# mLSTM heads of a hybrid decoder layer: column sums of a folded tile by transposes and a free-axis sum, in place of products with a constant

## The chip, the cores and the metric

The kernel runs on one core of one Trainium2 chip, in a single launch. The metric is device time in microseconds (us), from the start to the end of one execution; smaller is better.

## The reference, cut to what matters

One decoder layer on x of shape (1, 1024, 1024), everything in float32. Half of the first mixing stage is an mLSTM with four heads of width 128; the other half is an attention with forget gates (eight heads of width 64). Cross-attention, a squared-ReLU MLP and a last norm follow. The change lies in what each mLSTM head does at its end:

```python
den = scores.sum(-1) + inter * jnp.einsum('bhd,bhtd->bht', n, qc)
h = num / jnp.maximum(jnp.abs(den), jnp.exp(-m_t))[..., None]
...
mh = mh * lax.rsqrt(jnp.mean(mh * mh, axis=-1, keepdims=True) + EPS)
```

For each of the 1024 time steps a head needs two sums: one for the denominator `den`, one of the squares of the 128 numerators `num`. From them comes one factor for each time step, by which the numerators are multiplied.

## The kernel before, in words

The names: PE is the matrix engine (TensorE), DVE the VectorE, ACT the ScalarE, POOL the GpSimd, SP the queue that issues the transfers. Nearly every product is in float32 cut into two parts (`wh`, `wl` for weights, a pair of `act` tiles for data), and takes three matmuls (`mm3`, L221 to L223). PSUM has eight banks, of which three are called `sc`, two `tp`, and one each `mm`, `m2` (shown as `m`) and `ov`.

A head (`ml_head`, L630) works on two halves `hf` of 512 time steps, numerators lying with the channel on the partition and time on the free axis. For each half it goes over four blocks `j` of 128 keys: scores on PE into an `sc` bank (L655), a decay by ACT (`Exp`, L657) from a row `nmb` that was loaded into the tile `r_a` or `r_y`, a mask by POOL (L659), their product by DVE (L660), a cut of it into `r_d` (ACT, L138) and `r_e` (DVE, L139), the product with the values into the bank `ov` (L666), and a running sum of the denominators on POOL into `r_b` (L664). At the end of a half the sums over partitions are prepared by folding (L673 to L681): the tile `sq` (`r_a` for the first half, `r_y` for the second) holds on its partitions 0 to 63 the denominator terms, both halves of the partitions added, and on 64 to 127 the squares, added likewise. So the two sums wanted for each of 512 time steps are the sums over the lower and over the upper 64 partitions of `sq`.

`sums(hf)` (L636) takes them as four matmuls (one for each 128 time steps) with `sq` as the stationary operand and the constant `halves` [128, 2] as the moving one: column 0 of `halves` is one on the lower partitions, column 1 on the upper. The result is [128 time steps, 2] for each block, eight columns in one bank. ACT takes the absolute value of four of them into `dens` (L640), DVE copies the other four to `sqs` (L641). `sums(0)` is called in the loop of the second half, at j = 6, and `sums(1)` at the end. A dozen small instructions on DVE and one on POOL (L685 to L691, and L233 to L243) make the factor `c_fac` of it, 1024 values in 8 columns.

The rest is called the closing of the head. PE transposes `c_fac` (`to_row`, L285), ACT copies it out (L286), SP stores it in DRAM (`facd`) and loads it back, spread over all partitions, into `r_a` and `r_y` (L289, L696). DVE multiplies the numerators (tiles `r_f`) by it (L700) and by a gate (L701), ACT and DVE cut them, and the parts are stored to `mix` (L704, L705). The tiles are few: `r_a` and `r_y` have one buffer each, `r_f` two. So the next head's `nmb` can be loaded into `r_a` (L645) only when the closing before it has stored `mix` from `r_a`, and its numerators have no place until `r_f` is stored.

Between a head's `sums(1)` and its closing, and among the blocks of the next head, PE has the projections for the next head to do (`ml_project`: conv_silu, fx_project, gate; 24 matmuls of 512 columns each), and after the last head's projections the values of the attention (`token_major` on `w_fv`, 24 matmuls of 256 columns for each of eight tiles). The first stage takes from about 60 to 354 us of the span; then the slots of the attention follow.

The order of the instructions on each engine is not written out in this stage. The framework puts them in order while the program is built, by a timeline that it reckons for itself:

```python
with tile.TileContext(nc, schedule_with_timeline_sim=True) as tc:
```

From the attention's slots on (`in_order`) the order is fixed by the code. Each engine runs its list strictly in that order.

Of the kernel before, what the change touches and what calls it, by code (L numbers as in the profile page):

```python
# [11 lines left out]
AF = mybir.ActivationFunctionType  # L12
ALU = mybir.AluOpType
# [4 lines left out]
P = 128  # L18
# [26 lines left out]
def hybrid_layer(ctx: ExitStack, tc: tile.TileContext, a: dict, out: bass.AP):  # L45
    nc = tc.nc
    v, s, g = nc.vector, nc.scalar, nc.gpsimd
# [39 lines left out]
    def ps_tile(tag):  # L87
        return psum.tile([P, 512], F32, tag=tag, name=name(tag), bufs=PBUFS[tag])

    def sc():  # L90
        return ps_tile("sc")
# [4 lines left out]
    def ov_():  # L96
        return ps_tile("ov")
# [10 lines left out]
    def const(n, shape, dt=F32):  # L108
        return pool.tile(shape, dt, tag=n, name=n, bufs=1)
# [4 lines left out]
    ones = const("ones", [P, 1])  # L114
    g.memset(ones, 1.0)
    ident = const("ident", [P, P])
# [5 lines left out]
    g.affine_select(out=causal, in_=causal, pattern=[[-1, TH]], compare_op=ALU.is_ge, fill=-BIG, base=TH - P, channel_multiplier=1)  # L122
    half = const("half", [P, 8])
    g.memset(half, -0.5)
    halves = const("halves", [P, 2])
    g.memset(halves, 0.0)
    for e in range(2):
        g.memset(halves[e * (P // 2) : (e + 1) * (P // 2), e : e + 1], 1.0)
    vec = const("vec", [P, a["vec"].shape[1]])

    busy = ov_()
# [115 lines left out]
        for t in range(n):  # L247
            nc.tensor.matmul(ps[:, t * P : (t + 1) * P], cols[:, t : t + 1].broadcast_to([P, P]), ident, start=True, stop=True)

    def sum_cols(ps, src, n, by=ones):  # L250
        m = by.shape[1]
        for t in range(n):
            nc.tensor.matmul(ps[:, t * m : (t + 1) * m], src[:, t * P : (t + 1) * P], by, start=True, stop=True)

    def square_sum(acc, x, first, by=s, add=v):
        sq = acc if first else w2("c")[:, : x.shape[-1]]
# [88 lines left out]
    h = [(act(), act()), (act(), act())]  # L345
# [20 lines left out]
    for k in range(KT):  # L366
        if k == 1:
            load(wg_raw, a["w_gate"])
        if k % 2 == 0:
            c = slice(k % 4 * 256, k % 4 * 256 + 512)  # L370
# [39 lines left out]
    z, e, q, lf = (small[:, i:j].rearrange("p (t c) -> p t c", c=c) for i, j, c in ((0, 128, GC), (128, 224, GW), (224, 320, GW), (320, 416, GW)))  # L410
# [54 lines left out]
    ps = ov_()  # L465
# [92 lines left out]
    def quarter(e):  # L558
        return slice(e * HQ, e * HQ + HQ)
# [70 lines left out]
    def ml_head(hd, q, k, og, yq, state, late):  # L630
        fac = col("fac", 8)
        nums, folded = [], []
        dens = col("dens", 8)
        sqs = col("sqs", 8)

        def sums(hf):  # L636
            ps = sc()[:, 0:8]
            sum_cols(ps, folded[hf], 4, halves)
            ps = ps.rearrange("p (t e) -> p e t", e=2)
            s.activation(dens[:, 4 * hf : 4 * hf + 4], ps[:, 0], AF.Abs)  # L640
            v.tensor_copy(sqs[:, 4 * hf : 4 * hf + 4], ps[:, 1])  # L641

        for hf in range(2):
            nmb = w2("ay"[hf])
# [4 lines left out]
            for j in range(4 * hf, last + 1):  # L649
                d0 = j - 4 * hf  # L650
                c = quarter(d0 // 2)
# [17 lines left out]
                if j == 0:  # L669
                    e = w2("c", HQ)  # L670
# [6 lines left out]
            c = slice(0 if hf else HQ, TH)  # L677
# [7 lines left out]
        v.tensor_tensor(out=dens, in0=dens, in1=emc[:, :, hd], op=ALU.max)  # L685
        rd = col("rd", 8)
        v.reciprocal(rd, dens)
        v.tensor_tensor(out=sqs, in0=sqs, in1=rd, op=ALU.mult)
        v.tensor_tensor(out=sqs, in0=sqs, in1=rd, op=ALU.mult)
        rsqrt_cols(fac, sqs, 1.0 / P, 8)  # L690
        v.tensor_tensor(out=fac, in0=fac, in1=rd, op=ALU.mult)  # L691
# [82 lines left out]
    for _ in range(2):  # L774
        t = act().rearrange("p a b -> p (a b)").rearrange("p (i c) -> p i c", i=4)
# [272 lines left out]
    raws_, ages, cuts_, halves, last_raw = [], [], {}, [0], []  # L1048
# [139 lines left out]
    n = 0  # L1188
# [39 lines left out]
    for n0 in (0, 4):  # L1228
        ws = [weights(a["w_out_b"][n0 // 2 + i], 6 * P) for i in range(2)]
        for hf in range(2):  # L1230
            for n in range(n0, n0 + 4):
                w = both(ws[n // 2 % 2], lambda t: t.rearrange("p (k c) -> p k c", k=3)[:, :, n % 2 * P : n % 2 * P + P])
                ps = mm()
# [331 lines left out]
    for hd in range(XH):  # L1565
        q = query_blocks(hd)
        if hd == 0:
            t = act()
            for n in range(4):
                oh[n], ol[n] = t[:, n], t[:, 4 + n]  # L1570
        elif hd > 1:
            t = last_room if hd == 2 else right_room("-")
            t = t.rearrange("p q k c -> p (q k c)").rearrange("p (q n c) -> p q n c", q=2, n=2)
# [214 lines left out]
    for at, (b, m) in enumerate(steps):  # L1788
# [33 lines left out]
    for i in range(2):  # L1822
        t = act()
# [123 lines left out]
```

## Time and profile before

| | |
|---|---|
| median of 3 runs | 1497.02 us (1496.89 to 1497.15) |
| profiled execution | 1498.83 us, span of its instructions 1497.1 us |
| mean granted TensorE clock | 0.998 of full speed |
| busy | PE 99%, weight loads 84%, DVE 76%, ACT 52%, POOL 35% |

The profile is of one execution. Its views name groups by line, engine and operation, `out<-in` by the tile's names; times in a timeline are us from the start of the span. A matmul's recorded duration reaches beyond the start of the next one, since matmuls are pipelined; what a matmul costs is the distance between two starts. A matmul of two float32 operands appears as two records, a transposition as one.

### The profile page before, as it was taken

The page shows a single profiled execution, that of the slowest core. Times are in us where ns is not written, and L with a number is a line of the kernel's source. Part 1 is how long each engine was busy: PE and PEld are TensorE (multiplying, and loading weights), DVE is VectorE, ACT ScalarE, POOL GpSimd, SP SyncE. Part 2 cuts the span into 40 slices and gives each one's busy share as a digit, 9 for nine tenths or more (in the row PEclk, how much of TensorE's full clock was granted, in tenths as well). Part 3 has the DMA queues.
Part 4 walks back from the last instruction along what each step waited for, and adds up shares of the span by engine and source line. Part 5 has one row for each costly group of instructions (what it writes and reads, how often), then busy time and mean ns, then how long its engine had stood idle before and what let it go on. Part 6 is the DMA issues. An engine that isn't in the chain of part 4 may idle for free. (4 is left out here: it accounts for less than half of the span.)

```text
span 1497.1 us, 22496 instructions
## 1 busy us (share of the span) xinstructions
PE 1479.4 (99%) x7790; PEld 1253.1 (84%) x7790; DVE 1131.0 (76%) x1867; ACT 773.1 (52%) x1492; POOL 521.2 (35%) x552
## 2 busy tenths in 40 slices
PE   9999999999999999999999999999999999999997
PEld 9988888889999888889988787888888888888887
DVE  7775776776798875677668888999996677787665
ACT  7434353445688664577644557666665521222134
POOL 1002020414456441633200045454544365553312
PEclk9999999999999999999999999999999999999999
DMA  6422333446778867744544447776678767776623
GB/s 231 138 95 69 130 97 134 132 132 191 247 242 284 285 231 247 261 168 128 167 165 155 139 171 268 253 246 238 233 267 304 264 260 281 281 274 253 250 87 113
DMA packets 125878, 303.58 MB, mean 203 GB/s; under 512 B 14898, under 2 KB 30060, under 8 KB 118852
## 3 DMA queue, kind: packets, MB, share of 16 engines
q1 hardware_dynamic: 125764, 302.15, 57.9%
q8 instruction: 61, 1.00, 0.3%
q14 instruction: 53, 0.43, 0.1%
HBM read 203.28 MB, written 98.82 MB: 202 GB/s over the span
## 5 line engine op out<-in xcount | busy, mean ns | idle before, releaser
L221 PE MATMUL tp<-act,wl 128*128 128x512 f32 (+1 forms) x440 | 172.7, 392 | 0.0
L222 PE MATMUL tp<-act,wh 128*128 128x512 f32 (+1 forms) x440 | 172.2, 391 | 0.0
L223 PE MATMUL tp<-act,wh 128*128 128x512 f32 (+1 forms) x440 | 171.7, 391 | 0.0
L139 DVE TENSOR_TENSOR wl<-wr,wh 128x1024 fp32r<-128x1024 f32 (+2 forms) x99 | 131.8, 1331 | 29.0 <-ACT wh L138 28.7
L138 ACT ACTIVATE wh<-wr 128x1024 fp32r<-128x1024 f32 (+2 forms) x99 | 99.9, 1010 | 86.3 <-PE tp L223 28.9
L221 PE MATMUL mm<-act,wl 128*128 128x512 f32 (+1 forms) x332 | 123.7, 373 | 0.0
L223 PE MATMUL mm<-act,wh 128*128 128x512 f32 (+1 forms) x332 | 123.5, 372 | 0.0
L222 PE MATMUL mm<-act,wh 128*128 128x512 f32 (+1 forms) x332 | 123.5, 372 | 0.0
L221 PE MATMUL m<-act,wl 128*128 128x512 f32 (+1 forms) x308 | 113.9, 370 | 1.8 <-DVE wl L139 1.8
L223 PE MATMUL m<-act,wh 128*128 128x512 f32 (+1 forms) x308 | 113.7, 369 | 0.0
L222 PE MATMUL m<-act,wh 128*128 128x512 f32 (+1 forms) x308 | 113.4, 368 | 0.0
L223 PE MATMUL sc<-act,wh 128*128 128x512 f32 (+1 forms) x280 | 105.6, 377 | 0.0
L221 PE MATMUL sc<-act,wl 128*128 128x512 f32 (+1 forms) x280 | 105.5, 377 | 0.0
L222 PE MATMUL sc<-act,wh 128*128 128x512 f32 (+1 forms) x280 | 105.5, 377 | 0.0
L223 PEld LDWEIGHTS tp<-act,wh 128*128 128x128 f32 x440 | 82.7, 188 | 18.6
L221 PEld LDWEIGHTS tp<-act,wl 128*128 128x128 f32 x440 | 82.7, 188 | 18.5 <-DVE r_f L1627 0.2
L222 PEld LDWEIGHTS tp<-act,wh 128*128 128x128 f32 x440 | 82.8, 188 | 18.2
L1711 POOL TENSOR_TENSOR z<-wr 128x256 f32<-128x256 f32 x56 | 50.1, 915 | 135.6 <-DMA wr<-w_ff2q 133.1
L138 ACT ACTIVATE wh<-z 128x1024 fp32r<-128x1024 f32 (+1 forms) x54 | 55.4, 1026 | 79.0 <-POOL z L1711 58.4
L139 DVE TENSOR_TENSOR wl<-z,wh 128x1024 fp32r<-128x1024 f32 (+1 forms) x54 | 79.3, 1468 | 9.3 <-ACT wh L138 9.3
L138 ACT ACTIVATE w<-wr 128x768 fp32r<-128x768 f32 (+3 forms) x35 | 28.1, 802 | 109.5 <-PE tp L221 33.5
L223 PEld LDWEIGHTS mm<-act,wh 128*128 128x128 f32 x332 | 62.4, 188 | 11.7
(793 smaller groups left out, 4398.5 us busy)
## 6 DMA issues: line engine op xcount, KB each, us to landing
act<-right SPq DMA_DIRECT2D x49, 1024.0 KB
right<-w SPq DMA_DIRECT2D x56, 256.0 KB
wr<-w_ff2q SPq DMA_DIRECT2D x28, 512.0 KB
right<-r_d SPq DMA_DIRECT2D x49, 256.0 KB
right<-r_e SPq DMA_DIRECT2D x49, 256.0 KB
act<-fqk SPq DMA_DIRECT2D x48, 256.0 KB
wr<-w_in SPq DMA_DIRECT2D x20, 512.0 KB
wr<-w_ff SPq DMA_DIRECT2D x20, 512.0 KB
```

Of the source, the lines that this page charges most:

```text
L138: s.activation(hi, src, AF.Copy)
L139: return v.tensor_tensor(out=lo, in0=src, in1=hi.bitcast(F32), op=ALU.subtract)
L221: nc.tensor.matmul(ps, w[1], x[0], start=first, stop=False, skip_group_check=more)
L222: nc.tensor.matmul(ps, w[0], x[1], start=False, stop=False, skip_group_check=more)
L223: nc.tensor.matmul(ps, w[0], x[0], start=False, stop=last, skip_group_check=more)
L1711: g.tensor_tensor(out=o, in0=x, in1=y, op=op)
```

## The change

The constant `halves` goes. `sums` now transposes the four blocks of `sq` on PE into a whole `sc` bank, with the identity as the moving operand, so that time lies on the partitions and the 128 folded partitions on the free axis. One DVE instruction adds each run of 64 of the 512 columns of the bank into eight columns of a new tile `sums_`. ACT takes the absolute value from that tile, and the first product of the factor reads the squares' sums from it; the copy on DVE goes.

```diff
-    halves = const("halves", [P, 2])
-    g.memset(halves, 0.0)
-    for e in range(2):
-        g.memset(halves[e * (P // 2) : (e + 1) * (P // 2), e : e + 1], 1.0)
...
+        sums_ = sb("sums", [P, 16], 2).rearrange("p (h e t) -> p h e t", h=2, e=2)
         sqs = col("sqs", 8)
 
         def sums(hf):
-            ps = sc()[:, 0:8]
-            sum_cols(ps, folded[hf], 4, halves)
-            ps = ps.rearrange("p (t e) -> p e t", e=2)
-            s.activation(dens[:, 4 * hf : 4 * hf + 4], ps[:, 0], AF.Abs)
-            v.tensor_copy(sqs[:, 4 * hf : 4 * hf + 4], ps[:, 1])
+            ps = sc()
+            for t in range(4):
+                nc.tensor.transpose(ps[:, t * P : (t + 1) * P], folded[hf][:, t * P : (t + 1) * P], ident)
+            both_ = sums_[:, hf]
+            v.tensor_reduce(out=both_, in_=ps.rearrange("p (t e c) -> p e t c", e=2, c=P // 2), axis=mybir.AxisListType.X, op=ALU.add)
+            s.activation(dens[:, 4 * hf : 4 * hf + 4], both_[:, 0], AF.Abs)
...
-        v.tensor_tensor(out=sqs, in0=sqs, in1=rd, op=ALU.mult)
+        v.tensor_tensor(out=sqs.rearrange("p (h t) -> p h t", h=2), in0=sums_[:, :, 1], in1=rd.rearrange("p (h t) -> p h t", h=2), op=ALU.mult)
```

Since the order is reckoned anew, the lists of all engines differ between about 140 and 360 us of the span, though nothing there but `sums` is written otherwise. From the attention's slots on the lists are the same. Below, lists are of before and of the changed kernel, each row a line, an operation, and `out<-in`; lines after L630 stand five or three lower in the changed kernel (L285 is L280 there, L221 to L223 are L217 to L219).

The first place is DVE behind `sums(1)` of the third head (heads counted from one). Before, the copy, and the factor's small steps behind it, without a gap:

```order
L139 TENSOR_TENSOR r_d_2880<-ov_2869,r_d_2880 128x256
L641 COPY c_sqs_2523<-sc_2686 128x4
L685 TENSOR_TENSOR c_dens_2522<-c_dens_2522,emc 128x8
L687 RECIPROCAL c_rd_2694<-c_dens_2522 128x8
L688 TENSOR_TENSOR c_sqs_2523<-c_sqs_2523,c_rd_2694 128x8
L689 TENSOR_TENSOR c_sqs_2523<-c_sqs_2523,c_rd_2694 128x8
L233 TENSOR_SCALAR c_var_2698<-c_sqs_2523 128x8
L544 TENSOR_TENSOR z_443_2889<-tp_2917,row 128x512
```

In the changed kernel the same steps stand among wide instructions of the next head's projection:

```order
L637 TENSOR_REDUCE sums_2521<-sc_2685 128x8
L620 SCALAR_TENSOR_TENSOR r_b_3070<-z_449_2942,c_n_2860,r_c_3065 128x256 x2
L710 SCALAR_TENSOR_TENSOR r_p_3014<-tp_2989,row 128x512
L138 SCALAR_TENSOR_TENSOR act_2706<-z_449_2942,act_2706 128x1024
L599 TENSOR_TENSOR r_c_2965<-ov_2868,r_c_2965 128x128
L682 TENSOR_TENSOR c_dens_2520<-c_dens_2520,emc 128x8
L135 TENSOR_TENSOR wl_3409<-wr_3406,wh_3408 128x1024
L135 TENSOR_TENSOR r_p_3014<-r_p_3014,r_p_3016 128x512
L603 SCALAR_TENSOR_TENSOR r_c_2965<-r_c_2965,c_m_2707 128x128
L684 RECIPROCAL c_rd_2693<-c_dens_2520 128x8
```

What followed at once now follows with other work in between.

The second place is PE where it transposes the third head's `c_fac`. Before, this stands among the projections' matmuls of 512 columns, with 54 of them and 54 of 256 columns still to come ahead of the fourth head's first product into `ov`:

```order
L223 MATMUL mm_3028<-act_108,wh_2986 128x512
L285 MATMUL sc_2785<-ident,c_fac_2521 8x128
L221 MATMUL mm_3028<-act_108,wl_2987 128x512
L222 MATMUL mm_3028<-act_109,wh_2986 128x512
L223 MATMUL mm_3028<-act_108,wh_2986 128x512
```

In the changed kernel all matmuls of the projections are already ahead of it; it stands in the first tile of the attention's values (`mm_3412`), directly ahead of the fourth head's first scores, and 130 matmuls of 256 columns stand between it and the fourth head's first product into `ov`:

```order
L218 MATMUL mm_3412<-wl_3403,act_102 128x256
L280 MATMUL sc_2784<-ident,c_fac_2519 8x128
L217 MATMUL sc_3151<-act_2706 128x256
L218 MATMUL sc_3151<-act_2706 128x256
L219 MATMUL sc_3151<-act_2706 128x256
L217 MATMUL sc_3167<-act_2706,r_e_2977 128x256
```

The closing of the third head thus stands later in PE's list, and close to the fourth head's first scores.

The third place is PE at `sums(0)` of the fourth head. Before, it stands among the values' matmuls:

```order
L223 MATMUL tp_3557<-wh_3402,act_108 128x256
L221 MATMUL tp_3557<-wh_3402,act_109 128x256
L221 MATMUL ov_3230<-r_d_3271,act_111 128x256
L253 MATMUL sc_3279<-halves,r_a_3221 128x2 x2
L222 MATMUL ov_3230<-r_e_3272,act_111 128x256
L223 MATMUL ov_3230<-r_d_3271,act_111 128x256
L253 MATMUL sc_3279<-halves,r_a_3221 128x2 x2
```

In the changed kernel it stands behind a run of the fourth head's own scores and products, in which there is no other matmul:

```order
L217 MATMUL ov_3148<-r_d_3213,act_107 128x256
L218 MATMUL ov_3148<-r_e_3214,act_107 128x256
L219 MATMUL ov_3148<-r_d_3213,act_107 128x256
L217 MATMUL ov_3230<-r_d_3239,act_107 128x256
L218 MATMUL ov_3230<-r_e_3240,act_107 128x256
L219 MATMUL ov_3230<-r_d_3239,act_107 128x256
L217 MATMUL ov_3230<-r_d_3255,act_107 128x256
L218 MATMUL ov_3230<-r_e_3256,act_107 128x256
L219 MATMUL ov_3230<-r_d_3255,act_107 128x256
L635 MATMUL sc_3279<-ident,r_a_3221 128x128 x4
L217 MATMUL sc_3286<-act_2706 128x256
```

Between the transposed `c_fac` and this place there are 157 matmuls, all of 256 columns, where there were 54 of 512 and 155 of 256 columns. The run has moved together: what filled the spaces in it now stands ahead of it.

More of the change, by code (lines that the diff above doesn't have):

```diff
@@ L248, in spread, with sum_cols @@
             nc.tensor.matmul(ps[:, t * P : (t + 1) * P], cols[:, t : t + 1].broadcast_to([P, P]), ident, start=True, stop=True)
-    def sum_cols(ps, src, n, by=ones):
-        m = by.shape[1]
+    def sum_cols(ps, src, n):
         for t in range(n):
-            nc.tensor.matmul(ps[:, t * m : (t + 1) * m], src[:, t * P : (t + 1) * P], by, start=True, stop=True)
+            nc.tensor.matmul(ps[:, t : t + 1], src[:, t * P : (t + 1) * P], ones, start=True, stop=True)
     def square_sum(acc, x, first, by=s, add=v):
```

## The prediction

> **What bounds the kernel now.** I read the page's busy times first, then a table of stretches, then PE's timeline, then the chain from one head to the next.
>
> ```profile
> span 1497.1 us, 22496 instructions
> PE 1479.4 (99%) x7790; PEld 1253.1 (84%) x7790; DVE 1131.0 (76%) x1867; ACT 773.1 (52%) x1492; POOL 521.2 (35%) x552
> ```
>
> ```profile
> 60.00:180.00 120.00, 120.00 (x593) 99.32 (x592) 84.06 (x145) 48.65 (x88) 13.71 (x22) 1.00 0.30 93
> 240.00:300.00 60.00, 60.00 (x305) 50.17 (x304) 43.14 (x80) 28.46 (x52) 17.89 (x23) 1.00 0.43 144
> 300.00:354.00 54.00, 54.00 (x367) 49.54 (x367) 34.71 (x64) 25.06 (x52) 15.18 (x20) 1.00 0.48 151
> 360.00:680.00 320.00, 316.89 (x1918) 278.36 (x1917) 237.39 (x551) 215.41 (x548) 144.44 (x194) 1.00 0.71 239
> ```
>
> The columns are the stretch, its length, then the busy time of PE, PEld, DVE, ACT and POOL, the granted clock, the DMA share and GB/s. In the mLSTM stage (60 to 354) PE is busy all the time, in the attention behind it 99%. So work taken from PE in this stage shortens the span by as much, and a wait put into PE's list lengthens it by as much, and nothing behind it has room to give that back. Busy PE could hide waits, since ends of matmuls are modelled; but going through the starts one by one from 60 to 354 I find none that is late. PE's list has its work just where it is ready.
>
> **The part on PE.** The four matmuls of `sums` and four transpositions of the same kind (L586, also from a float32 tile with the identity) as they stand in PE's timeline, each with what follows:
>
> ```profile
> 143.50 0.39 PE L221 MATMUL tp<-act,wl 128*128 128x512 f32 x1
> 143.73 0.95 PE L253 MATMUL sc<-halves,r_a 128*128 128x2 f32 x8
> 144.53 0.36 PE L221 MATMUL sc<-w,w 128*128 128x256 f32 x1
> 154.08 0.60 PE L586 MATMUL tp<-ident,r_b 128*128 128x128 f32 x4
> 154.44 0.48 PE L222 MATMUL m<-act,wh 128*128 128x512 f32 x1
> ```
>
> From first start to the next instruction: 144.53 - 143.73 = 0.80 us for eight records with 2 columns, 154.44 - 154.08 = 0.36 us for four with 128. Columns cost little here, passes cost. Gain 0.44 for each group; 4 heads x 2 halves = 8 groups: **-3.5 us**, between -3.4 and -3.7 by the rounding of the rows.
>
> **The part on DVE and ACT.** A copy of eight columns goes, a sum over 512 columns of a PSUM bank comes; the attention has one of that size.
>
> ```profile
> L641 DVE COPY c_sqs<-sc x8: 147/155/164, 145.6 to 353.9; 128x4 f32<-128x4 f32 x8
> L822 DVE TENSOR_REDUCE c_mx<-sc x32: 667/680/693, 358.3 to 551.5; 128x1 f32<-128x512 f32 x32
> ```
>
> 0.68 - 0.16 = 0.52 us more, eight times: 4.2 us more on DVE, which is busy 43 of 60 us here. The direct cost is nothing as long as PE has other matmuls; that cover is the next term. The Trainium skill, "VectorE: DVE Perf Modes", section "Rules for kernel authors", speaks against the change: it expects the reduction at one element a cycle, calls it the slowest VectorE operation on a hot path and advises to restructure. By that rule, if DVE were the path, the sum would be -3.5 + 4.2 = +0.7 us; the row's duration agrees, but the table above does not show DVE as the path. The three memsets of `halves` leave POOL at the start, where nothing waits for them: 0.
>
> **The part that moves.** The chain between two heads is long and serial, and I take its length from the third head's closing into the fourth head:
>
> ```profile
> 309.74 0.28 PE L285 MATMUL sc<-ident,c_fac 128*8 128x128 f32 x1
> ...
> 315.29 0.75 DVE L700 SCALAR_TENSOR_TENSOR r_f<-r_f,vec,r_a 128x512 f32<-128x512 f32 x1 [0.91 <-DMA r_a<-facd]
> ...
> 318.14 0.64 ACT L141 ACTIVATE r_a<-r_f 128x512 fp32r<-128x512 f32 x1 [5.10 <-DVE r_f L701]
> 325.44 0.51 ACT L657 ACTIVATE r_b<-r_a,gcol 128x256 f32<-128x256 f32 x1 [5.51 <-DMA r_a<-rows]
> ...
> 326.65 1.05 ACT L138 ACTIVATE wh<-wr 128x1024 fp32r<-128x1024 f32 x1
> ...
> 328.13 0.40 ACT L138 ACTIVATE r_d<-r_b 128x256 fp32r<-128x256 f32 x1
> ...
> 328.82 0.28 PE L221 MATMUL ov<-r_d,act 128*128 128x256 f32 x1
> ...
> 338.17 1.29 POOL L681 TENSOR_TENSOR r_a<-r_a,r_b 128x512 f32<-128x512 f32 x1
> ...
> 340.76 0.50 PE L253 MATMUL sc<-halves,r_a 128*128 128x2 f32 x4
> ```
>
> `c_fac` leaves PE at 309.74, goes through DRAM, the numerators are scaled and stored, and only then `r_a` is loaded with the next head's row: ACT starts the fourth head at 325.44, 15.7 us later, having waited for that transfer. From there POOL's fold, which `sums(0)` needs, ends at 338.17 + 1.29 = 339.46, 14.0 us later. Together 29.7 us, in which PE had 340.76 - 309.74 = 31.0 us of work. The other closings give the spread of the first leg and of the second:
>
> ```profile
> 176.41 0.28 PE L285 MATMUL sc<-ident,c_fac 128*8 128x128 f32 x1
> ...
> 191.72 0.51 ACT L657 ACTIVATE r_b<-r_a,gcol 128x256 f32<-128x256 f32 x1 [5.47 <-DMA r_a<-rows]
> ...
> 206.28 1.30 POOL L681 TENSOR_TENSOR r_a<-r_a,r_b 128x512 f32<-128x512 f32 x1
> ...
> 245.15 0.27 PE L285 MATMUL sc<-ident,c_fac 128*8 128x128 f32 x1
> ...
> 259.80 0.51 ACT L657 ACTIVATE r_b<-r_a,gcol 128x256 f32<-128x256 f32 x1 [2.07 <-DMA r_a<-rows]
> ...
> 261.54 0.40 ACT L138 ACTIVATE r_d<-r_b 128x256 fp32r<-128x256 f32 x1
> ```
>
> First leg 15.3 and 14.65; second leg 207.58 - 191.72 = 15.9 for the second head.
>
> In the changed list there are 157 matmuls of 256 columns between that `c_fac` and the fourth head's `sums(0)`. Their distance:
>
> ```profile
> 350.14 0.28 PE L222 MATMUL tp<-wl,act 128*128 128x256 f32 x1
> ...
> 352.14 0.28 PE L221 MATMUL tp<-wh,act 128*128 128x256 f32 x1
> ```
>
> 17 steps in 2.00 us, 0.118 each; so the cover is 157 x 0.118 = 18.5 us where it was 31.0. PE must wait for the rest, first ahead of the scores and the first `ov` of the fourth head, then between its blocks, then at `sums(0)`. With this head's own legs the wait is 29.7 - 18.5 = 11.2 us. The chain itself can be shorter than before: ACT's cut at 326.65 (1.05 us) and other work of the projections no longer stands ahead of the first `r_d` in ACT's changed list, and I grant 1 us for that. The low end takes the fastest first leg (14.65) and 2 us off the second: 14.65 + 12.0 - 18.5 = 8.2; the high end the slowest of both, 15.7 + 15.9 - 18.5 = 13.1. I take **+10.2 us**, nearest to this head's rows.
>
> Behind `sums(0)` 80 rows follow up to `sums(1)`, 9.4 us. The chain there begins with the last block's L660 and ends with the fold on DVE:
>
> ```profile
> 343.91 0.42 DVE L660 SCALAR_TENSOR_TENSOR r_c<-sc,r_c 128x256 f32<-128x256 f32 x1
> ...
> 349.52 0.69 DVE L681 TENSOR_TENSOR r_y<-r_y,r_b 128x512 f32<-128x512 f32 x1 [0.88 <-ACT r_b L680]
> ...
> 352.26 0.95 PE L253 MATMUL sc<-halves,r_y 128*128 128x2 f32 x8
> ```
>
> From 343.91 to 350.21 it is 6.3 us, and about 1.5 us for the scores and the sum on DVE ahead of it (an estimate from the 0.68 above and the starts on PE): covered; `sums(1)`, at 352.26 before, moves with `sums(0)`. The two earlier transitions keep their cover: from `c_fac` to the first `ov` there are 72 matmuls of 512 and 18 of 256 columns, then 75 and 11, or 18.9 and 18.8 us at 0.23 (143.50 to 143.73 is such a step) and 0.118; needed are 328.13 + 0.40 - 309.74 = 18.8 at most, 261.54 + 0.40 - 245.15 = 16.8 at least. I set 0 to 0.5 us, and 0 in the sum.
>
> Sum: -3.5 + 10.2 = **+6.7 us**. The profiled execution took 1498.83 us, 1.7 around its span of 1497.1, and stands 1.8 above the median; so it would become 1505.5, and the median 1497.02 + 6.7 = **1503.7 us**.
>
> **Rivals.** What counts as no change here is 0.2%, 3.0 us: 1494.0 to 1500.0.
>
> - The gain alone: if the 18.5 us hold the chain after all (the two legs would have to fall to 18.5 together, far below any row), only -3.5 is left: 1493.5. For it: the transfers are light at that place and the lists ahead of them shorter. Against it: the legs repeat within 1 us at three heads. It decides where the wait falls below 0.5 us; 1 in 10, which also holds what I misread in the order.
> - DVE as the path, or a wait that is partly given back: the rule above, 1497.7 by the rows. For it: the sums' chain gets longer by 0.52 in each half. Against it: no wait of PE's for DVE in the stage. 0.12.
> - The wait also lowers the clock. At its start the kernel shows what slow matmuls cost, and the longest wait of PE in the middle shows that 2.1 us do no harm:
>
> ```profile
> 1.96 1.44 PE L133 MATMUL ov<-ident 128*128 128x128 f32 x5 [1.96 <-POOL ident L118]
> ...
> 645.61 0.39 PE L221 MATMUL sc<-w,r_c 128*128 128x256 f32 x1 [2.12 <-DVE r_c L142]
> ```
>
> Five of those first matmuls take 1.44 us, about 0.2 apart, against 0.36 / 4 = 0.09 for the transpositions of L586. If a wait of several us brings this back for some 5 us, about 2.5 us are lost: 1506.2. The Trainium skill, "TensorE: Matmul & The Clock Gate", section "Why this matters for your kernels", says so: gaps of more than about 3 us put the clock back to half. No wait so long stands in the middle of this trace, so it neither agrees nor differs. 0.16.
> - More than the sum: weights (512 KB) are queued between the stores and loads of the closing, and earlier transitions fall behind too: above 1508.5, 0.04.
>
> **How the numbers follow.** The forecast itself, the wait at the fourth head with the clock kept (1501.7 to 1506.6 by 8.2 and 13.1), has 0.58. Slower by over 0.2%: 0.58 + 0.16 + 0.04 = 0.78; within: 0.12; faster: 0.10. The range leaves out the gain alone, about half of the second rival and the last: 1497.5 to 1508.5.
>
> **What would show it.** Right: eight groups of transpositions 0.36 us long; PE idle about 10 us between the third head's `c_fac` (309.74 + 54 x 0.23 - 6 x 0.44, near 320 us) and the fourth head's `sums(0)`, released by ACT, DVE and the fold on POOL; `sums(1)` of that head near 359 us instead of 352.26; all later stretches as long as before. Wrong: PE busy without a gap from 300 to 354, or gaps at the earlier heads; a first leg shorter than 14 us; a clock below 1.00 behind the gap.

## The result and the profile after

| | before | changed |
|---|---|---|
| median of 5 runs, us | 1497.02 | 1513.13 |
| lowest to highest, us | 1496.48 to 1497.15 | 1511.49 to 1515.70 |
| profiled execution, us (span) | 1498.83 (1497.1) | 1513.13 (1511.4) |
| granted clock, mean | 0.998 | 0.994 |

The changed kernel takes 1.011 times as long as before [1.0096, 1.0124]: slower by 16.1 us, where 6.7 were forecast. The head of the page, and the same table of stretches as before, but with the last one from 380 us on, since the attention begins later:

```profile
span 1511.4 us, 22420 instructions
PE 1484.4 (98%) x7758; PEld 1253.0 (83%) x7758; DVE 1135.8 (75%) x1867; ACT 772.8 (51%) x1492; POOL 526.3 (35%) x549
```

```profile
60.00:180.00 120.00, 120.00 (x588) 99.01 (x587) 85.56 (x145) 48.27 (x86) 13.72 (x22) 1.00 0.31 95
240.00:300.00 60.00, 58.46 (x283) 48.08 (x283) 41.63 (x76) 26.86 (x49) 19.67 (x23) 1.00 0.42 139
300.00:354.00 54.00, 48.68 (x284) 41.92 (x284) 32.12 (x62) 21.01 (x43) 10.56 (x17) 0.93 0.32 99
380.00:680.00 300.00, 298.15 (x1793) 261.29 (x1792) 223.96 (x523) 203.29 (x515) 135.92 (x184) 1.00 0.74 249
```

PE was busy without a gap up to 354 us before. Now 1.5 us are missing from 240 to 300 and 5.3 from 300 to 354, and there the clock is below 1. PE's timeline at the third head's last sums, its `c_fac`, and the fourth head's two sums:

```profile
307.52 0.60 PE L635 MATMUL sc<-ident,r_y 128*128 128x128 f32 x4
307.88 0.48 PE L218 MATMUL tp<-act,wh 128*128 128x512 f32 x1
...
323.48 0.27 PE L280 MATMUL sc<-ident,c_fac 128*8 128x128 f32 x1
...
352.01 1.05 PE L635 MATMUL sc<-ident,r_a 128*128 128x128 f32 x4
352.71 0.56 PE L217 MATMUL sc<-act 128*128 128x256 f32 x1
...
363.88 0.60 PE L635 MATMUL sc<-ident,r_y 128*128 128x128 f32 x4
364.23 0.36 PE L812 MATMUL sc<-act 128*128 128x256 f32 x1
```

The groups last 0.36 us from start to next start, as forecast, except the one at 352.01: 0.70, that is half the clock. `c_fac` leaves PE at 323.48 (309.74 before), `sums(0)` stands at 352.01 (340.76), `sums(1)` at 363.88 (352.26). What PE waited for from 330 to 366 us (engine, tile and line, the releaser, us in all, times, the longest):

```profile
PE tp L217 <- DVE r_f L617: 1.5, 1, 1.5
PE ov L217 <- DVE r_f L675: 1.0, 1, 1.0
PE ov L217 <- ACT r_d L134: 1.0, 1, 1.0
PE ov L218 <- DVE r_e L135: 0.9, 2, 0.6
```

No wait is long; there are many, and behind 346 us the products run at half speed. The clock records of the trace give half clock from 346.17 to 356.40 us, and nowhere else between the start and the end of the kernel:

```profile
335.00:346.17 11.17, 8.18 (x55) 6.70 (x54) 4.83 (x11) 4.29 (x10) 3.50 (x7) 1.00 0.36 121
346.17:356.40 10.23, 7.91 (x31) 6.76 (x31) 6.50 (x14) 6.62 (x15) 7.76 (x11) 0.50 0.22 62
```

The stretches of the mLSTM stage, of the changed kernel and then the one of before that belongs to the third row:

```profile
180.00:260.00 80.00, 79.15 (x390) 65.61 (x389) 52.93 (x94) 31.94 (x60) 14.62 (x19) 1.00 0.35 111
260.00:300.00 40.00, 38.46 (x190) 31.74 (x189) 31.44 (x57) 21.58 (x41) 16.82 (x21) 1.00 0.47 156
335.00:355.00 20.00, 14.68 (x78) 12.06 (x78) 10.62 (x23) 10.43 (x24) 9.91 (x16) 0.78 0.25 81
```

```profile
335.00:355.00 20.00, 19.75 (x168) 19.41 (x166) 10.51 (x27) 10.51 (x24) 10.45 (x11) 1.00 0.60 177
```

From 335 to 355 PE does 78 products in place of 168. To add it up I took each PE start to the next, less the usual distance for its columns (0.231 us for 512, 0.116 for 256, 0.109 for 128 and fewer): what is left over is time lost, by waits or by the clock. Of the 10.9 us in the third row, 5.5 were lost ahead of 346.17, at full clock, and 5.4 behind it.

| stretch, us | before | changed | difference |
|---|---|---|---|
| 180 to 260 | 0.8 | 1.9 | +1.1 |
| 260 to 300 | 0.4 | 2.3 | +1.9 |
| 334 to 354 | 0.3 | 10.9 | +10.6 |
| 354 to the attention's first products (358.8, 370.4) | 2.0 | 4.1 | +2.1 |

That is 15.7, less 3.5 for the groups 12.2; by the starts of the same product of the attention (357.37 before, 369.07 after) the stage lost 11.7. The rest of the way, by the same comparison of starts: +10.0 us at 904 before (two old waits at 643 and 856 have shrunk by 1.3 and 1.0), +13.3 at 1100, +13.8 at the last product (1490.7), and 14.3 by the spans. So some 3.3 us were lost between 904 and 1100, in the feed-forward part, whose lists are unchanged. The last 1.8 of the 16.1 are no loss: the profiled execution before stood that far above its median.

### The profile page after: what moved, and what is told of

The parts are those of the page before. It is cut to its first block, busy times and chain, and to the rows that moved or that the text cites. A ratio compares the mean times of both kernels' runs of the same rounds, so it can differ in the third digit from the quotient of the medians.

```text
span 1511.4 us, 22420 instructions
## 1 busy us (share of the span) xinstructions
PE 1484.4 (98%) x7758; PEld 1253.0 (83%) x7758; DVE 1135.8 (75%) x1867; ACT 772.8 (51%) x1492; POOL 526.3 (35%) x549
## 4 chain that ended last, share of the span: by engine, by line
PE 83%; DVE 7%; DMA 5%; ACT 2%; issue 2%; POOL 1%; SPq 0%; DVEq 0%; POOLq 0%; ACTq 0%
PE tp L217 7%; PE tp L218 7%; PE tp L219 7%; PE sc L217 6%; PE sc L218 5%; PE sc L219 5%; PE m L217 5%; PE m L219 5%; PE m L218 5%; PE mm L217 5%; PE mm L218 5%; PE mm L219 5%; PE ov L879 2%; PE tp L860 2%; PE ov L218 2%
## 5 line engine op out<-in xcount | busy, mean ns | idle before, releaser
L217 PE MATMUL tp<-act,wl 128*128 128x512 f32 (+1 forms) x440 | 172.6, 392 | 0.4 <-DVE r_f L1624 0.4
L219 PE MATMUL tp<-act,wh 128*128 128x512 f32 (+1 forms) x440 | 171.8, 391 | 0.0
L217 PE MATMUL mm<-act,wl 128*128 128x512 f32 (+1 forms) x332 | 123.7, 372 | 1.1 <-DVE r_f L1624 1.1
L219 PE MATMUL mm<-act,wh 128*128 128x512 f32 (+1 forms) x332 | 123.3, 371 | 0.0
L217 PE MATMUL m<-act,wl 128*128 128x512 f32 (+1 forms) x308 | 114.0, 370 | 0.6 <-DVE wl L135 0.6
L219 PE MATMUL m<-act,wh 128*128 128x512 f32 (+1 forms) x308 | 114.0, 370 | 0.0
L217 PE MATMUL sc<-act,wl 128*128 128x512 f32 (+1 forms) x280 | 105.7, 377 | 1.2 <-DVE r_f L1624 1.2
L219 PE MATMUL sc<-act,wh 128*128 128x512 f32 (+1 forms) x280 | 105.6, 377 | 0.0
L217 PEld LDWEIGHTS tp<-act,wl 128*128 128x128 f32 x440 | 82.7, 188 | 19.4 <-DVE r_f L1624 0.9
L219 PEld LDWEIGHTS tp<-act,wh 128*128 128x128 f32 x440 | 82.7, 188 | 18.5
L217 PEld LDWEIGHTS mm<-act,wl 128*128 128x128 f32 x332 | 62.4, 188 | 12.5 <-DVE r_f L1624 1.5
```

The lines of the kernel that those rows point to most:

```text
L217: nc.tensor.matmul(ps, w[1], x[0], start=first, stop=False, skip_group_check=more)
L219: nc.tensor.matmul(ps, w[0], x[0], start=False, stop=last, skip_group_check=more)
```

## The experiments

My theory was that the order costs and the operations do not. The order of a kernel can be held: at the end of the program every instruction of an engine is chained to the one ahead of it in a table (its rank in the program, by place in the list). Both kernels have the same instructions in each list, one for one, except for the three memsets of `halves` on POOL, which stand first and are left out of the chain. So a table of one fits the other.

```
+    for e_, tab in ORDERS.items():
+        eng = getattr(mybir.EngineType, e_)
+        traced = [i for i in nc.cur_bb.bb.instructions if i.engine == eng]
...
+        for x, y in zip(tab, tab[1:]):
+            tc.add_manual_dep(traced[y], traced[x].name, mybir.DependencyInfo(mybir.DependencyClass.NoSync, mybir.DependencyReason.DATA), reason="the table")
```

All results, with the ratio to the kernel before on the same chip (its median there is 1496.6 us for e1 to e4, 1497.1 for e5 to e8, 1496.9 for e9 and e10, 1496.6 for e11 and e12). The ratio is estimated from all runs and need not be the quotient of the medians:

| run | median, us | ratio [95%] |
|---|---|---|
| e1_old_order | 1501.67 | 1.0031 [1.0021, 1.0042] |
| e2_new_order | 1512.69 | 1.0106 [1.0093, 1.0119] |
| e3_transposes_alone | 1500.81 | 1.0021 [1.0012, 1.0030] |
| e4_sum_alone | 1499.14 | 1.0017 [1.0009, 1.0026] |
| e5_before_60_fewer | 1500.29 | 1.0019 [1.0010, 1.0028] |
| e6_64_more | 1497.09 | 0.9998 [0.9990, 1.0007] |
| e7_first_two_new | 1509.52 | 1.0084 [1.0070, 1.0097] |
| e8_sum_ahead | 1498.21 | 1.0006 [0.9997, 1.0016] |
| e9_sum_ahead_56_more | 1495.22 | 0.9993 [0.9983, 1.0003] |
| e10_pe_order_alone | 1499.96 | 1.0017 [1.0008, 1.0026] |
| e11_wide_fill | 1496.27 | 1.0000 [0.9991, 1.0009] |
| e12_wide_and_tiny_fill | 1501.92 | 1.0037 [1.0025, 1.0050] |

### Order and operations apart: e1, e2, e10

e1_old_order is the changed kernel with before's table on all engines, e2_new_order the kernel before with the changed kernel's table, e10_pe_order_alone as e1 with PE's table alone.

> The changed operations, with every engine's list (TensorE, ScalarE, VectorE, GpSimd and the transfers that SyncE issues) held in the order that the kernel before had; nothing is left out. Theory (the lists' order costs, the operations do not): the groups' gain alone, 8 x 0.44 = 3.5 us, so 1493 to 1494.5 us, no idle TensorE time around 335 to 353 us, and a granted clock of 0.998. Rival 1 (the operations cost: the longer VectorE sum delays the factor chain and what is queued behind it): no better than before, 1497 to 1501 us, with TensorE waiting for VectorE at the sums. Rival 2 (the waits in the feed-forward part near 992 to 1113 us belong to the changed operations): 1495.5 to 1497 us, with these waits in the trace.

> The operations of the kernel before (products with halves, a copy), with every engine's list in the order that the changed kernel has. Theory (the order costs): the loss of the changed kernel without the groups' gain, 1512 to 1517 us, with the run of waits around 335 to 353 us and a granted clock of about 0.994. Rival 1 (the operations cost, the order is harmless): 1496.5 to 1498 us. Rival 2 (half by order, half by operations): about 1505 us.

> The changed operations, with TensorE's list alone held in the old order; the other engines' lists are the scheduler's own. Theory (what costs is that TensorE takes projections ahead of the heads' own products): as e1_old_order, 1497 to 1504 us. Rival (the places in VectorE's or ScalarE's list cost by themselves): 1506 us or more.

e2 decides the main point: the old operations in the new order lose 16.1 us. That this is as much as the change loses is partly chance, since e2 has neither the groups' gain nor the later loss in the feed-forward part: at 380 us of before its starts are 15.1 us behind, 3.4 more than those of the changed kernel, and from 904 to 1100 it loses nothing more (13.4 and 13.3). Its table of stretches has the same hole:

```profile
260.00:300.00 40.00, 39.61 (x198) 32.94 (x197) 31.38 (x57) 21.84 (x41) 16.83 (x21) 1.00 0.47 156
335.00:355.00 20.00, 13.91 (x78) 11.50 (x77) 9.93 (x22) 9.86 (x24) 9.26 (x16) 0.89 0.25 79
355.00:375.00 20.00, 18.14 (x117) 17.15 (x116) 10.36 (x32) 10.18 (x27) 10.45 (x11) 0.77 0.69 218
```

e10 shows that it is enough to hold PE's list: the scheduler then puts everything else within some 8 places of before by itself, and the hole is gone. What the other engines' new lists would cost with PE's old one was not run. But e1 missed its 1493 to 1494.5: the hole is gone, at 349 us its starts are 3.65 us ahead of before, as the groups' gain says, and yet its median is 5 us above before. e1's profile is of its fastest run (1496.93, mean clock 0.998). It shows two places where the changed operations cost something behind the mLSTM stage; the 4.7 us from there to its median stand in no trace. The first place is PE's waits from 340 to 375 us, with VectorE's timeline there:

```profile
PE sc L821 <- ACT w L843: 1.4, 1, 1.4
PE sc L821 <- DVE sums L646: 1.1, 1, 1.1
```

```profile
349.96 1.22 DVE L144 TENSOR_TENSOR wl<-wr,wh 128x1024 fp32r<-128x1024 f32 x1 [0.61 <-ACT wh L143]
351.10 0.68 DVE L646 TENSOR_REDUCE sums<-sc 128x8 f32<-128x512 f32 x1
```

The last group was on PE at 349.06; its sum stands behind a split that nothing wants yet, and holds the score bank until 351.8. The attention's third score needs this bank. The wait for ACT (1.6 us before) stays. The second place lies far behind: PE waits of 1.3 and 1.6 us near 977 and 1037 us, as in the changed kernel.

### The two halves of the change: e3, e4

```
-            v.tensor_reduce(out=both_, in_=ps.rearrange("p (t e c) -> p e t c", e=2, c=P // 2), axis=mybir.AxisListType.X, op=ALU.add)
-            s.activation(dens[:, 4 * hf : 4 * hf + 4], both_[:, 0], AF.Abs)
+            ps = ps.rearrange("p (t e c) -> p e t c", e=2, c=P // 2)[:, :, :, 0]
+            s.activation(dens[:, 4 * hf : 4 * hf + 4], ps[:, 0], AF.Abs)
+            v.tensor_copy(both_[:, 1], ps[:, 1])
```

This is e3_transposes_alone, from the changed kernel. e4_sum_alone adds to the kernel before, ahead of its copy:

```
+            v.tensor_reduce(out=sums_[:, hf], in_=folded[hf].rearrange("p (t e c) -> p e t c", e=2, c=P // 2), axis=mybir.AxisListType.X, op=ALU.add)
```

> Only TensorE's half of the change: four transposes in place of the four products, but VectorE copies and ScalarE takes one column of each 64 in place of their sum (the sums are left out). The lists are ordered anew by the scheduler: the third head's factor transposition stands 9 rows later on TensorE than before, where the whole change has it 67 rows later. Theory: the groups' gain, less up to 0.5 us for the 9 rows, 1493 to 1495 us. Rival (transposes themselves cost, by their PSUM bank or by the clock): above 1497 us, with waits at the score banks.

> Only VectorE's half of the change, as an addition: the products with halves and the copy stay, and VectorE also sums the 512 columns of the folded tile (from SBUF; its result is used nowhere). The lists are ordered anew: the third head's factor transposition stands 9 rows later on TensorE. Theory: eight sums of about 0.6 us are covered on VectorE, 1496.5 to 1498 us. Rival (VectorE's longer list delays the factor chains): 1500 us or more, with TensorE waiting for VectorE in the transitions between heads.

Neither half brings the big loss: the scheduler moves the third head's `c_fac` by 9 rows for each half and by 67 for both. Both missed their forecast upwards. e3, like e1, has the feed-forward waits (1.6, 0.8 and 0.3 us) and the bank's wait (1.4), and the clock at 0.86 from 348 to 360 us. e4 has no feed-forward wait; its loss of 2.5 us is small and only partly found: the clock is at 0.83 from 355 to 365 us, and its starts are 0.1 us behind those of before at 357.4 and 1.1 at 380.

### The feed-forward part: e5, e6

The waits near 977, 1037 and 1100 us came with three kernels (changed, e1, e3) and not with three others (before, e2, e4), in one and the same order of all lists there. What the first three have in common is that `halves` is gone, which moves the addresses of the tiles behind it, and that PE has 64 instructions fewer (32 loads, 32 products). ACT's waits from 955 to 1130 us, before, changed and e1, name a transfer:

```profile
ACT r_p L1640 <- DMA right<-r_p: 0.2, 1, 0.2
```

```profile
ACT r_p L1637 <- DMA right<-r_p: 4.8, 3, 1.9
```

```profile
ACT r_p L1646 <- DMA right<-r_p: 3.9, 2, 2.0
```

This store is queued behind a load `z<-w_ff`. The table of transfer queues shows one more user of the transfer engines, blocks of code (packets, MB, share of 16 engines). The first row is the whole kernel before, the second its stretch 961 to 967 us, the third, of the changed kernel, the stretch 976 to 982:

```profile
q8 instruction: 61, 1.00, 0.3%
```

```profile
q8 instruction: 1, 0.02, 1.0%
```

```profile
q8 instruction: 1, 0.02, 2.5%
```

1.0% of 16 engines in 6 us is 0.96 us for the block, 2.5% is 2.4 us: the block itself takes longer when it meets the load. 61 blocks of 16 KB for 15,696 TensorE records (loads, products and waits) are 257 records each, so I take this queue for TensorE's code. The Trainium skill, "Runtime: NRT & Kernel Launch", section "Instruction fetch mechanics", says the same, 16 KiB blocks of 256 instructions by a DMA queue of the engine's own, and calls the cost mostly hidden. PE itself never waits for its code here; what pays is the load that the block meets.

```
-    for _ in range(15):
+    for _ in range(0):
         nc.tensor.matmul(busy[:, :P], ident, ident, start=True, stop=True)
```

e5_before_60_fewer is the kernel before without these idle products at the start, `halves` kept, order held. e6_64_more is e1 with idle transpositions where PE waits, behind the second and the third score of the attention's first head:

```
+            if self.hd == 0 and self.i in (1, 2):
+                idle = ps_tile("ov")
+                for n in range(16):
+                    extra.append(nc.tensor.transpose(idle[:, 4 * n : 4 * n + 4], ident[0:4], ident[0:4, 0:4]).ins.name)
```

> The kernel before (products with halves), every list in its own order, without the 15 idle TensorE products at the start, which is 60 fewer TensorE instructions (load and multiplication of two records each); nothing that is used is left out. The traces so far show TensorE's instructions fetched in blocks of 16 KB, about one each 256 instructions, through the same 16 transfer engines as the data; the changed groups have 64 fewer instructions in all, and the block that arrived near 962 us, 5 us ahead of a load z<-w_ff of 512 KB before, arrives 1 us after that load's start in the profile of e1_old_order, where the load landed after 5.8 us in place of 3.8 and TensorE lost 1.5 and 1.7 us. Theory (the instruction count moves the fetches onto the loads): these waits near 977, 1037 and 1097 us appear in this kernel too, 2 to 4 us in all, so 1498 to 1502 us with up to 2 us at the start either way. Rival (the tile halves of 32 bytes in a partition, whose removal moves the addresses of all tiles behind it, is the cause): no such waits, 1495 to 1499 us.

> The changed kernel in the old order (as e1_old_order), with 2 x 16 idle transpositions of 4 columns in a free bank added on TensorE ahead of the third and fourth scores of the first attention head, where TensorE waited 1.1 and 1.4 us in e1_old_order; that is 64 instructions more, as many as the change took away. Theory (the count of instructions moves their fetches onto the loads, and the waits lower the clock): no waits near 977 to 1100 us, no half clock near 355 us, 1493 to 1496.5 us. Rival 1 (addresses): the waits in the feed-forward part stay, 1497 to 1502 us. Rival 2 (the runs of e1_old_order above 1500 us have another cause than waits and clock here): 1500 us or more.

Both came out as the count of instructions says, against the addresses. The stretch 960 to 1120 us of before, changed, e5 and e6:

```profile
960.00:1120.00 160.00, 160.00 (x687) 128.65 (x686) 148.18 (x158) 105.97 (x166) 78.50 (x49) 1.00 0.70 243
```

```profile
960.00:1120.00 160.00, 157.27 (x673) 125.84 (x672) 144.70 (x154) 103.10 (x162) 75.63 (x48) 1.00 0.67 234
```

```profile
960.00:1120.00 160.00, 157.67 (x674) 126.17 (x673) 143.98 (x155) 103.41 (x162) 76.17 (x48) 1.00 0.69 240
```

```profile
960.00:1120.00 160.00, 159.81 (x686) 128.29 (x685) 147.88 (x157) 103.62 (x162) 78.50 (x49) 1.00 0.70 245
```

PE is short of 2.7 us in the changed kernel, of 2.3 in e5, of 0.2 in e6. From the traces' transfer records, for the load `z<-w_ff` near 967 us of before: when the nearest block of code began (us from the load's issue), and how long the load took to land:

| kernel | block of code | load landed after |
|---|---|---|
| before, e4, e6, e9, e12, e2 | -5.0, -4.9, -5.0, -5.1, -4.4, -6.4 | 3.8, 3.7, 3.8, 3.9, 3.8, 3.8 |
| changed, e1, e5 | +1.2, +1.0, +1.0 | 5.7, 5.8, 5.9 |
| e3, e7, e8, e10 | +3.7, +3.0, +3.4, +3.2 | 5.8, 6.4, 5.5, 5.5 |
| e11, here and at its load near 1079 | -3.1 and +1.5 | 3.9 and 5.9 |

The block that comes while this load is on its way adds some 2 us to it. The records say more: a transfer has sixteen landings, and in the collisions of the table fifteen of the load's sixteen came within 3.9 us, as before; only one came after 5.5 to 6.4. That fits one transfer engine held up by the block, which is one packet; which engine carried it is not recorded. The store behind has a late sixteenth part too, ACT's next `r_p` and VectorE's addition wait, and PE waits 2.1 to 3.7 us in up to three places, 60 us apart (1.3 in e11). At the second place the late part is that of a load `wr<-w_ff` or of the store behind it (in the changed kernel 5.6 us, its other parts 4.2).

The offset alone does not decide: near 1082 to 1097 us seven of these kernels (changed, e1, e3, e5, e7, e8, e10) have a block 3.4 to 3.7 us behind such a load, and the load lands after 3.9 to 4.2 us. By the count of instructions the fourteen traces are in order: with none or 8 fewer than before no PE wait above 0.2 us there, with 34 fewer one (e11), with 60 or 64 fewer two or three.

e6's median is not 1493 to 1496.5 but 1497.1: in its profile the clock is 0.83 from 350 to 360 us in spite of the filled waits.

### Where the new order loses: e7

e7_first_two_new has the changed kernel's tables up to the third head's own rows and before's from there. The kernel holds the finished tables; this is how they were joined:

```
+    CUT = dict(PE=1351, Activation=227, DVE=322, Pool=62, SP=114)
+    ORDERS = {e: new[e][:c] + old[e][c:] for e, c in CUT.items()}
```

> The changed operations with the new order in the first two transitions between heads and the old order from the third head's own rows on (on every engine). Theory (the third head's late factor transposition is nearly the whole loss): as e1_old_order or up to 1.5 us above it, 1498 to 1503.5 us. Rival (the new order loses at every transition): 1504 to 1508 us.

The rival won: 1509.5. With the new order in the first two transitions alone the starts at 346 us are 5.4 us later than before, 8.6 more than in e1. The loss stands where the old order begins again (PE's waits from 255 to 300 us, and the stretch):

```profile
PE sc L226 <- DVE r_b L666: 1.8, 1, 1.8
PE mm L226 <- DVE r_f L626: 1.6, 1, 1.6
PE ov L227 <- DVE r_e L144: 0.7, 1, 0.7
```

```profile
260.00:275.00 15.00, 10.92 (x41) 8.45 (x40) 8.61 (x18) 6.73 (x16) 5.01 (x10) 0.77 0.43 133
```

So the third head's late `c_fac` is the end of something longer. In the new order PE takes projections ahead of the heads' own products at each transition. That costs little there (1.1 us from 180 to 260 in the changed kernel); the head falls behind. The changed kernel's `c_fac` leave PE 3.1, 6.6 and 13.7 us later than before (179.53, 251.73, 323.48 against 176.41, 245.15, 309.74), while the groups should bring them earlier. The lag is paid where no projections are left to take: in e7 in the third head, in the changed kernel in the fourth. One thing is not separated: e7 joins two lists that the scheduler never put together, so the join itself can be part of its 8.6 us. The other half, the old order first and the new one from the third head on, was not run.

### What is left to win: e8, e9, e11, e12

e8_sum_ahead exchanges two neighbours in VectorE's table of e1 (shown decoded): the last sum (rank 435) goes ahead of the split (464).

```
-    "DVE": [..., 459, 464, 435, 436, ...],
+    "DVE": [..., 459, 435, 464, 436, ...],
```

> As e1_old_order, but the last head's last VectorE sum stands one place earlier in VectorE's list, ahead of a split of 1024 columns (1.22 us) that is not wanted yet. Theory: TensorE's wait of 1.1 us for the score bank falls to under 0.3 us, and with it the half clock behind it comes more rarely: 1 to 3 us under e1_old_order's median of 1501.7, so 1498 to 1501 us; the waits near 977 to 1100 us stay. Rival (that wait covers another that ends as late, the ScalarE exponential): no gain, 1501 to 1503 us.

The 1.1 us wait is gone, and the ratio falls from e1's 1.0031 to 1.0006; the wait for ACT remains:

```profile
PE sc L821 <- ACT w L843: 1.6, 1, 1.6
```

The other three fill this wait with idle work behind the third score of the first attention head, which also sets the count of instructions (`extra` keeps these instructions out of the table):

```
+            if self.hd == 0 and self.i == 2:
+                idle = ps_tile("ov")
e9:
+                for n in range(28):
+                    extra.append(nc.tensor.transpose(idle[:, 4 * n : 4 * n + 4], ident[0:4], ident[0:4, 0:4]).ins.name)
e11, and e12 with the last two lines:
+                for n in range(15):
+                    extra.append(nc.tensor.matmul(idle[:, :256], qs2[:, it], kl[:, :256], start=True, stop=True).ins.name)
+                    if n < 13:
+                        extra.append(nc.tensor.transpose(idle[:, 256 + 4 * n : 260 + 4 * n], ident[0:4], ident[0:4, 0:4]).ins.name)
```

> As e8_sum_ahead (changed operations, old order, the last sum ahead of the split), with 28 idle transpositions of 4 columns in a free bank on TensorE ahead of the fourth score of the first attention head, where e8_sum_ahead still waited 1.76 us: 56 instructions more, of the 64 that the change took away. Theory (what is left of the gain is lost to fetches that meet loads, and to the clock after that wait): no waits near 977 to 1100 us, the clock full from 350 to 360 us, 1493.5 to 1496 us, under the kernel before. Rival (another loss that no profile so far shows): 1496.5 us or more.

> As e8_sum_ahead, with 15 idle products of 256 columns (30 instructions) in a free bank ahead of the fourth score, in place of the 28 transpositions of 4 columns of e9_sum_ahead_56_more, behind which the 256-column products had gone at a pitch of 0.213 us for 3.5 us where 0.118 is usual. Theory (a wait filled with tiny instructions counts as idle for the clock, one filled with wide ones does not): full clock from 350 to 360 us, 1.5 us won there against e9; and TensorE's blocks of code, 34 instructions or 3.9 us later in the work than before, end about as the load near 962 us begins, so the waits in the feed-forward part are under 1.5 us in all: 1493 to 1496 us. Rival (the half clock comes by what went before the wait): 0.213 us again, 1495 to 1498 us.

> As e11_wide_fill, with 13 idle transpositions of 4 columns between the 15 wide products, 56 instructions in all as in e9_sum_ahead_56_more. They last about 0.8 us longer than the wait. Theory: full clock, and no waits near 977 to 1100 us, 1492.5 to 1495.5 us, under the kernel before. Rival (half clock again, or the fetches meet other loads): 1496 us or more.

The stretches around the fill, of e9, e11 and e12:

```profile
348.00:353.00 5.00, 5.00 (x52) 4.67 (x51) 4.04 (x14) 3.94 (x11) 1.27 (x1) 0.97 0.46 125
353.00:358.00 5.00, 5.00 (x29) 4.72 (x29) 4.04 (x16) 2.29 (x9) 3.70 (x5) 0.69 0.59 184
```

```profile
348.00:353.00 5.00, 5.00 (x41) 4.78 (x39) 4.28 (x14) 4.11 (x13) 1.29 (x1) 1.00 0.53 118
353.00:358.00 5.00, 5.00 (x40) 4.71 (x39) 4.67 (x18) 2.61 (x10) 3.70 (x5) 1.00 0.62 189
```

```profile
353.00:358.00 5.00, 5.00 (x19) 3.46 (x20) 1.36 (x8) 0.89 (x4) 2.40 (x3) 0.79 0.58 172
358.00:363.00 5.00, 5.00 (x22) 4.61 (x22) 3.12 (x12) 2.09 (x7) 1.74 (x3) 0.53 0.28 97
```

In these profiles the clock stays full behind the wide products and goes to half behind the tiny transpositions, though PE counts as busy in both. That is one profile each, and it is no rule: six of e9's eleven runs have a mean clock of 0.998, as before's profile has, and only three of e11's. The two fills also differ in kind, transposition or product, and not in width alone. e11 keeps the clock and pays 1.3 us at one collision (its load near 1079, table above); e9 has no collision and pays for the clock. In e12 each pair of a wide product and a tiny transposition took 0.46 us at full clock, where the two take 0.18 in runs of their own, and 0.71 us once the clock was at half (from 355.9). So the fill lasted 7.1 us (351.16 to 358.26) where I had reckoned 2.6: a miss. e9's median is 1.7 us under the kernel before, and e11's equals it; no interval lies below 1, so a version that beats the kernel before is not shown. Nothing recovers the whole 3.5 us: e9's profiled execution is 3.8 us ahead at the last product, but against a profile of before that is itself 1.8 us above its median.

## Why the prediction was wrong, point by point

- **The groups, -3.5 us.** Right: 0.36 us each on PE (307.88 - 307.52), and e1 is 3.65 us ahead at 349 us.
- **VectorE's sum, 0.** Its duration was right (0.68 us), its cover for seven of the eight. The last sum stands behind a split, and PE waits for its bank: 1.1 us in the old order (e1, undone in e8), and 1.7 in the changed kernel, at 366.85, where before waited 1.6 for ACT. e2, with the old copy at that place, waits 1.9, so in the new order the longer operation is not what sets this wait (the changed kernel, then e2):

```profile
PE sc L812 <- DVE sums L637: 1.7, 1, 1.7
PE sc L824 <- DVE c_sqs L650: 1.9, 1, 1.9
```

The rule that made VectorE the path would have given 1497.7; PE's other waits in the stage are for the heads' chains, not for the sums.

- **The wait at the fourth head, +10.2 us.** Right in place; that the size agrees (10.6 between 334 and 354 us) is partly luck. I had priced a wait at full clock, from legs of 15.7 and 13.0 us. In the changed kernel the first leg took 15.9 us (323.48 to 339.40), and the second 11.7, less than my low end:

```profile
339.40 0.51 ACT L654 ACTIVATE r_b<-r_a,gcol 128x256 f32<-128x256 f32 x1 [5.61 <-DMA r_a<-rows]
...
349.81 1.27 POOL L678 TENSOR_TENSOR r_a<-r_a,r_b 128x512 f32<-128x512 f32 x1
```

The fold ends at 351.08, and `sums(0)` starts 0.9 us later, behind PE's own products at half clock. So waits and half clock made up the 10.6 together, about half of it behind 346.17; what the wait would have been at full clock is not shown. And its cause reaches further back than the one list place I named: `sums(1)` of the third head is itself 12 us late (307.52 against 295 before).

- **The earlier transitions, 0.** This step failed, in the way that the prediction had named as a sign of being wrong: 3.0 us were lost there (180 to 300), and the third `c_fac` stands at 323.48 where I had put it near 320. e7 shows that the new order of these transitions alone costs 8.6 us against e1; how much of the changed kernel's later wait is this lag is argued from it, not measured. I counted the cover from `c_fac` to the next head's first product, head by head, and not how late each head already was.
- **The clock.** The forecast kept it at full speed, and this failed too; I had it as a rival at 0.16, for one wait of several us. It came: half clock from 346.17 to 356.40 us, 0.78 from 335 to 355, with no wait above 1.5 us, and it makes up part of the 10.6 and 1.0 of the 2.1 behind it (up to 356.40). The Trainium skill, "TensorE: Matmul & The Clock Gate", section "A second HAM failure mode: psum-queue depth-cycling", tells of short gaps between groups that set the clock back, and this trace agrees; the rule of gaps above 3 us, which I used, does not cover it.
- **"All later stretches as long as before".** This failed too: +3.3 us from 904 to 1100, by 64 instructions fewer on TensorE (e5, e6). Nothing in the lists could show it, since the lists there are the same.
- **The sum.** -3.5 + 10.6 + 3.0 + 2.1 = 12.2 by lost time, 11.7 by the starts, in place of 6.7; then -1.7 up to 904, +3.3 up to 1100, +1.0 to the end: 14.3 by the spans. From median to median it is 1.8 more, because the profiled execution of before stands that far above its median, which I noted and left out of the range.

What stays open: how much of the lag's price is waiting and how much the clock, and how much of each unprofiled run is the clock. e1's runs go from 1496.9 to 1504.2 us with a mean clock of 0.998 in the lowest and 0.994 to 0.997 in the others, but only one run has a profile.

## What to carry to other kernels

Where a scheduler sets the order, price the order of a change apart from its operations: hold the old list with the new operations and the new list with the old ones. A chain that falls behind is a debt: follow its lateness through all repetitions up to where the filling work ends, rather than its cover at one place. When lists and operations of a stage are the same and its time is not, look at what else shares the transfer engines, code included. A sum that comes out right can hide two terms that are wrong: look at the legs as well as at the total.

## What the runs showed of the hardware

- TensorE's code comes in blocks of 16 KB, one for 257 records, through the engines that carry the data. In eight traces a block that began 1.0 to 3.7 us behind the issue of a 512 KB load went with one of its sixteen parts landing after 5.5 to 6.4 us, where the other fifteen kept to 3.9; at another load, 3.4 to 3.7 us did no harm. 60 or 64 instructions fewer, 600 to 960 us earlier in the program, brought this about (2.1 to 3.7 us of PE's waits), and 64 more took it away.
- The clock goes to half without a long gap: no wait above 1.5 us from 335 to 355 us, but a quarter of the time idle (14.68 of 20 us busy), and the clock at 0.78. A single wait of 1.6 us (e8), and two of 1.1 and 1.4 (e1), left it at full speed in the profiles. Between the start and the end of the kernel, half clock lasts 3.41, 6.83 or 10.24 us in all eight traces that have it, by their clock records.
- A stretch that counts as busy can still be followed by half clock: 28 transpositions of 4 columns in e9's profile (5.00 of 5 us busy, clock 0.69 behind them). 15 products of 256 columns in their place kept 1.00 in e11's; over all runs the two do not differ so.
- A product of 256 columns and a transposition of 4 in turns take 0.46 us a pair, 2.5 times what they take in runs of their own (0.120 in e11 and 0.062 in e9).
